# Keys and values of the memory attention, made within the input projection instead of among the scans

## The chip, the core and the metric

One core of one Trainium2 chip runs the whole kernel. The metric is the device time of one execution in microseconds; the time before is the median of three runs. TensorE multiplies matrices and has two levels of clock, 1.2 and 2.4 GHz; the profile gives what was granted as a share of the higher. VectorE (DVE in the rows), ScalarE (ACT) and GpSimd (POOL) do the elementwise work, SyncE (SP) issues most of the transfers. Each engine executes its instructions in an order that is fixed when the kernel is built, and waits by semaphores.

## The reference, cut to what matters

One layer of an encoder: 2048 tokens of width 1024. One input projection feeds a state space mixer (S5: per group of 16 channels a diagonal recurrence forwards and backwards over the sequence) and the queries of a cross-attention into 256 memory tokens. Both outputs go through one output projection and a layer norm, then through a mixture of 16 experts.

```python
def _memory_attention(q_mem, mem, w_kv):
    kv = (mem @ w_kv).reshape(bsz, mem.shape[1], 2, MEM_HEADS, MEM_HEAD_DIM)
    q = q_mem.reshape(bsz, L, MEM_HEADS, MEM_HEAD_DIM)
    s = jnp.einsum('blhd,bmhd->bhlm', q, kv[:, :, 0]) * (MEM_HEAD_DIM ** -0.5)
    p = jax.nn.softmax(s, axis=-1)
    out = jnp.einsum('bhlm,bmhd->blhd', p, kv[:, :, 1])
    return out.reshape(bsz, L, MEM_WIDTH)
...
proj = x @ s5_w_in[j]
mix = _s5_mixer(proj[..., :S5_WIDTH], ...)
mem_out = _memory_attention(proj[..., -MEM_WIDTH:], mem, mem_w_kv[i])
y = jnp.concatenate([mix, mem_out], axis=-1) @ w_out
```

The change concerns `mem @ w_kv`: 256 memory tokens by 1024, times 1024 by 512 (256 columns of keys, 256 of values). It depends on no token of the sequence.

## The kernel before, in words

Every float32 product is made of three f16 matmuls (`mm3`, L106 to L110): each operand is split into a high half (a cast, on ScalarE) and a low half (the difference to it). `split_w` (L90) makes the low half on VectorE, and scales a weight by 64 while it does so. `split_w_pool` (L95) does the same with ScalarE and GpSimd: a cast on ScalarE, a scaling in place on ScalarE, and a subtraction on GpSimd.

`front` runs these stages:

- **Input projection** (`inproj_u`): 16 tiles of 128 tokens. Per tile a load `xr` (SyncE), a cast `xh` (ScalarE), a difference `xl` (L262: GpSimd for tiles 1 to 5, VectorE otherwise), 24 matmuls into `pu` and 48 into `pq`, both with one PSUM buffer; `pu` is evicted by ScalarE (L281), `pq`, the queries, by ScalarE and VectorE (L294, L295, rows `OT<-pq`). The tables of the recurrence are made in between: `s5_base` behind tile 0, nearly all of it small VectorE instructions (names `b_...`, `pwa`, `turn`), `scan_base` behind tile 6 (names `E`), and `s5_block(b)` behind every second tile, on GpSimd (`wtmp`, L576) and VectorE (`wz` in PSUM, L580; `wi` and `wo`, L581). A block's kernel matrix goes through PSUM tag `pk`, which has one buffer, and ScalarE reads it out (L616, `ks<-pkk`). After tiles 7 and 15 the columns are transposed by TensorE into the chunk columns `U` (L301, evicted at L304 and L306). Before that, `U`'s memory takes the raw input weights. The `U` half of tiles 0 to 7 is written first, the other one after the last tile.
- **Scans**: eight blocks of four groups, in the order 6, 7, 0 to 5. `chunk_inputs(b)` multiplies `U` by stored matrices (L638, `pvv`) and ScalarE evicts them (L641, `S<-pvv`); `scan(b)` turns the states (`turn_states`: L690 on VectorE, L691 on GpSimd, L695 on either), scans them on VectorE (L715), turns them back, and ScalarE copies them out in eight instructions (L720, `SS<-S`). Behind the first two blocks stands `kv(att, t)`: it loads the memory (`mraw`, L347) and `w_kv` (`kraw`, L354) in pieces, splits them with ScalarE and VectorE (L348, L349, L91, L92), runs 96 matmuls, and writes keys and values as f16 halves `kh`, `kl`, `vh`, `vl` (L366 to L378).
- **Attention and S5 output**: the order on TensorE is written out by hand (`manual_schedule`, `STEPS`): the outputs of blocks 0 and 1, then attention steps (scores L734, exponentials L740 on ScalarE, probabilities, values) between the outputs of the other blocks.
- Then the gated unit, the output projection with norm and routing, and the experts.

Apart from TensorE's hand-written stage, the framework sets the order on each engine when the kernel is built: it walks through the program with a timeline of estimated durations and takes what is ready, the earlier in the program first. So an instruction can move past others on its engine, but on the chip that order doesn't change any more. Buffers of one PSUM tag are given out in program order. The lines ahead of the prediction's steps:

```python
for b in order[:KEEP]:
    self.scan(b)
self.kv(att, t)
...
for b in order[KEEP:]:
    self.chunk_inputs(b, [self.stored(b, q, wip) for q in range(GB // 2)], self.ps1, "s5")
    self.scan(b)
```

Of the kernel before, what the change touches and what calls it, by code (L numbers as in the profile page):

```python
# [18 lines left out]
P = 128  # L19
# [3 lines left out]
DC = 8  # L23
# [15 lines left out]
XG = 9  # L39
GTB = 1  # L40
GELU = 6

EARLY = 2
EARLY_T = 10
# [19 lines left out]
WS = 64.0  # L64
# [8 lines left out]
class Kern:  # L73
# [97 lines left out]
    def front(self, fr):  # L171
# [17 lines left out]
        with ExitStack() as s5:  # L189
            up = s5.enter_context(self.pool("up", side="left"))  # L190
            self.U = up.tile([P, 2, G, P], F32, name="U")
            att = s5.enter_context(self.pool("att", side="left"))
            with ExitStack() as t0:
                self.inproj_u(t0, scp)
            ssp = s5.enter_context(self.pool("ssp", side="left"))
            self.SS = ssp.tile([P, 2, G, P + 2], F32, name="SS")
            self.nc.gpsimd.memset(self.SS[:, 0, :, 0:1], 0.0)
            self.nc.gpsimd.memset(self.SS[:, 1, :, P + 1:P + 2], 0.0)
            with ExitStack() as t2:
                self.ps1 = t2.enter_context(self.pool("ps1", bufs=3, space=PSUM))  # L200
                self.ps2 = t2.enter_context(self.pool("ps2", bufs=1, space=PSUM))
                order = list(range(NB - KEEP, NB)) + list(range(NB - KEEP))
                gtp = t2.enter_context(self.pool("gtp", bufs=GTB, side="left"))
                wp = [t2.enter_context(self.pool("wopa", bufs=2, side="left"))]
                with ExitStack() as t:
                    self.scp = t.enter_context(self.pool("scm", bufs=2, side="right"))
                    for b in order[:KEEP]:
                        self.scan(b)
                    self.kv(att, t)
                    wip = t.enter_context(self.pool("wip", bufs=WIP, side="right"))  # L210
                    for b in order[KEEP:]:
                        self.chunk_inputs(b, [self.stored(b, q, wip) for q in range(GB // 2)], self.ps1, "s5")
                        self.scan(b)
                steps = self.attention(t2)
                gup = t2.enter_context(self.pool("gup", bufs=2, side="right"))
                wp.append(t2.enter_context(self.pool("wopb", bufs=2, side="right")))
                with self.tc.manual_schedule(engines={mybir.EngineType.PE}):
                    counts = iter(STEPS)
                    for b in range(NB):
                        if b == GELU:  # L220
                            self.glu_weights()
                        for _ in self.s5_out(b, gtp, wp, gup):
                            for _ in range(next(counts)):
                                next(steps, None)
                    for _ in steps:
                        pass
# [9 lines left out]
        self.xk = [keep.tile([P, D], F32, name=f"xk{e}") for e in range(EARLY)]  # L236
        self.outproj()

    def inproj_u(self, t0, scp):
# [15 lines left out]
        for t in range(NT):  # L255
# [52 lines left out]
            if t == 0:  # L308

                self.PRb = ps.tile([P, 16, 2, G], F32, tag="pw", bufs=1, name="PRb")  # L310
                self.s5_base(t0)
                nc.scalar.activation(self.PRb, self.PR[:, 1:17], AF.Copy)
                self.blkp = t0.enter_context(self.pool("s5blk", side="right"))
            if t == 6:
                self.scan_base(scp)
            if t % 2 == 1 and t < NT - 1:
# [15 lines left out]
                    f(n - k)  # L332
                yield

    def kv(self, att, t):
        nc, a = self.nc, self.a
        ps = self.ps2
        kp = t.enter_context(self.pool("kvp", bufs=2, side="right"))
        self.kh = att.tile([P, 4, 256], F16, name="kh")
        self.kl = att.tile([P, 4, 256], F16, name="kl")  # L340
        self.vh = att.tile([P, 2, 256], F16, name="vh")
        self.vl = att.tile([P, 2, 256], F16, name="vl")
        mh = kp.tile([P, DC, 256], F16, bufs=1, name="memh")
        ml = kp.tile([P, DC, 256], F16, bufs=1, name="meml")
        for c in range(0, DC, 4):
            m = kp.tile([P, 4, 256], F32, tag="raw", name=f"mraw{c}")
            nc.sync.dma_start(m, a["memT"][:, c:c + 4])  # L347
            nc.scalar.activation(mh[:, c:c + 4], m, AF.Copy)  # L348
            nc.vector.tensor_tensor(ml[:, c:c + 4], m, mh[:, c:c + 4], op=ALU.subtract)  # L349
        kacc = [ps.tile([P, 512], F32, tag="at", bufs=3, name=f"pk{k}") for k in range(2)]  # L350
        vacc = [ps.tile([P, 512], F32, tag="pS", bufs=2, name=f"pv{k}") for k in range(2)]
        for c2 in range(0, DC, 2):
            raw = kp.tile([P, 2, 512], F32, tag="raw", name=f"kraw{c2}")
            nc.sync.dma_start(raw, a["w_kv"][:, c2:c2 + 2])  # L354
            wh = kp.tile([P, 2, 512], F16, tag="kvh", bufs=1, name=f"kvh{c2}")
            wl = kp.tile([P, 2, 512], F16, tag="kvl", bufs=1, name=f"kvl{c2}")
            self.split_w(wh, wl, raw)
            for i in range(2):
                c = c2 + i
                ends = c == 0, c == DC - 1  # L360
                for k in range(2):
                    sl = slice(k * P, k * P + P)
                    self.mm3(kacc[k][:, :256], wh[:, i, sl], wl[:, i, sl], mh[:, c], ml[:, c], *ends)
                    self.mm3(vacc[k][:, :256], mh[:, c, sl], ml[:, c, sl], wh[:, i, 256:], wl[:, i, 256:], *ends)
        for k in range(2):
            nc.scalar.activation(self.vh[:, k], vacc[k][:, :256], AF.Copy, scale=1.0 / WS)  # L366
            nc.vector.scalar_tensor_tensor(self.vl[:, k], vacc[k][:, :256], 1.0 / WS, self.vh[:, k], op0=ALU.mult, op1=ALU.subtract)
            th = kp.tile([P, 2, 512], F16, tag="kvh", bufs=1, name=f"kth{k}")[:, 0, :256]
            tl = kp.tile([P, 2, 512], F16, tag="kvl", bufs=1, name=f"ktl{k}")[:, 0, :256]
            nc.scalar.activation(th, kacc[k][:, :256], AF.Copy, scale=1.0 / WS)  # L370
            nc.vector.scalar_tensor_tensor(tl, kacc[k][:, :256], 1.0 / WS, th, op0=ALU.mult, op1=ALU.subtract)

            for hh in range(2):
                r = slice(hh * 64, hh * 64 + 64)
                for half in range(2):
                    o = slice(half * 64, half * 64 + 64)
                    nc.scalar.activation(self.kh[o, k * 2 + hh], th[r], AF.Copy)
                    nc.scalar.activation(self.kl[o, k * 2 + hh], tl[r], AF.Copy)  # L378


    def s5_base(self, t0):
# [1210 lines left out]
```

## Time and profile before

| | |
|---|---|
| median of three runs (lowest, highest) | 1093.69 us (1084.93, 1095.92) |
| the profiled execution | 1091.53 us |
| its span in the profile | 1089.7 us |
| TensorE busy in the span | 899.5 us, 83% |
| VectorE | 828.3 us, 76% |
| ScalarE | 540.5 us, 50% |
| GpSimd | 535.3 us, 49% |

The shares are means over stages with different limits, so the rows below go by stage. The input projection runs from the start to about 226 us, the scans from there to 337 us, the attention to about 540 us. A row of the timeline has the start, the time that the instruction took, its engine, line, operation, what it writes from what, and in brackets how long its engine was idle before it and what ended that. A duration holds what the instruction was held up once it had begun, so the same shape can have two durations.

### The profile page before, as it was taken

How to read it: one execution, taken by the hardware profiler on the slowest of the kernel's cores; microseconds unless marked ns; L12 is line 12 of the kernel's file. 1: busy time of each engine (PE TensorE's matmuls, PEld its weight loads, DVE VectorE, ACT ScalarE, POOL GpSimd, SP SyncE). 2: the span in 40 equal slices, each digit the busy share in tenths (PEclk: the TensorE clock that was granted, in tenths of full speed). 3: DMA queues.
4: the chain of work that ended last, by engine and by line, in shares of the span. 5: the costliest groups of instructions: out<-in, count | busy, mean ns of one | idle time of the engine just before them, and what ended most of it. 6: DMA issues, size and time to landing. Idle time of an engine off the chain costs nothing. (4 is left out here: it accounts for less than half of the span.)

```text
span 1089.7 us, 18757 instructions
## 1 busy us (share of the span) xinstructions
PE 899.5 (83%) x7108; PEld 606.8 (56%) x7108; DVE 828.3 (76%) x1636; ACT 540.5 (50%) x1068; POOL 535.3 (49%) x379
## 2 busy tenths in 40 slices
PE   7777599985845999899999888698979987989880
PEld 4444465674734877444554447476657754755540
DVE  7999888969997666483585676467878787878774
ACT  5122243445748776477633312265656554746530
POOL 1475655426663331325945444525444566367454
PEclk9899799999887999999999987899999998999995
DMA  7113355275271422417736331476578669557531
GB/s 253 41 45 117 121 180 202 69 243 168 61 227 46 132 81 77 140 55 267 257 141 116 78 114 64 142 292 227 206 269 319 215 225 334 198 205 233 208 107 65
DMA packets 65199, 178.14 MB, mean 163 GB/s; under 512 B 15121, under 2 KB 33425, under 8 KB 57681
## 3 DMA queue, kind: packets, MB, share of 16 engines
q1 hardware_dynamic: 44800, 128.83, 36.2%
q0 software_dynamic: 20304, 48.07, 12.9%
q8 instruction: 57, 0.93, 0.3%
q14 instruction: 38, 0.30, 0.1%
HBM read 141.95 MB, written 58.49 MB: 184 GB/s over the span
## 5 line engine op out<-in xcount | busy, mean ns | idle before, releaser
L92 DVE SCALAR_TENSOR_TENSOR wl<-raw,wh 128x1024 f16<-128x1024 f32 x82 | 97.8, 1219 | 10.4 <-ACT wh L91 7.9
L91 ACT ACTIVATE wh<-raw 128x1024 f16<-128x1024 f32 x82 | 82.0, 1048 | 24.1 <-PE pg L109 13.8
L109 PE MATMUL pg<-xl,wh 128*128 128x288 f16 (+1 forms) x256 | 73.3, 288 | 3.0 <-DVE xl L1462 2.8
L110 PE MATMUL pg<-xh,wl 128*128 128x288 f16 (+1 forms) x256 | 73.3, 288 | 0.9 <-issue 0.9
L108 PE MATMUL pu<-xh,wh 128*128 128x288 f16 (+1 forms) x256 | 71.8, 283 | 2.4 <-DVE hl L1049 1.9
L108 PE MATMUL pg<-xh,wh 128*128 128x288 f16 (+1 forms) x256 | 73.5, 289 | 0.0
L1206 POOL DMA_INDIRECT xs<-xg,idxall x31 | 38.9, 1256 | 70.2 <-DVE xg L1499 40.9
L110 PE MATMUL pu<-xh,wl 128*128 128x288 f16 (+1 forms) x256 | 71.6, 282 | 1.5 <-issue 1.5
L109 PE MATMUL pu<-xl,wh 128*128 128x288 f16 (+1 forms) x256 | 71.6, 282 | 0.0
L109 PEld LDWEIGHTS <-wh 128*128 128x128 f16 x576 | 58.1, 101 | 19.0 <-issue 5.7
L108 PEld LDWEIGHTS <-wh 128*128 128x128 f16 x576 | 58.3, 101 | 18.5 <-issue 3.5
L110 PEld LDWEIGHTS <-wl 128*128 128x128 f16 x576 | 57.9, 101 | 17.5 <-issue 4.4
L108 PE MATMUL pq<-xh,S 128*128 128x128 f16 x256 | 51.0, 235 | 15.9 <-DVE OT L295 15.9
L743 POOL TENSOR_TENSOR pe<-pe,ri 128x1024 f32<-128x1024 f32 x16 | 30.3, 1895 | 55.5 <-DVE ri L742 38.8
L108 PE MATMUL pu<-winh,xh 128*128 128x512 f16 x128 | 49.7, 388 | 6.6 <-ACT winh L91 6.6
L1201 POOL DMA_INDIRECT xg<-x1d,idxall x31 | 37.9, 1222 | 32.9 <-DMA out_x<-xg,idxall 13.0
L108 PE MATMUL py<-wh,hh 128*128 128x512 f16 x120 | 45.9, 385 | 8.8 <-ACT hh L1048 4.6
L1462 DVE TENSOR_TENSOR xl<-pt,xh 128x512 f16<-128x512 f32 x60 | 39.5, 683 | 16.1 <-ACT xh L1461 10.1
L1461 ACT ACTIVATE xh<-pt 128x512 f16<-128x512 f32 x60 | 34.0, 592 | 35.8 <-PE pt L1458 29.5
L110 PE MATMUL pq<-xh,S 128*128 128x128 f16 x256 | 51.2, 235 | 0.4 <-DVE S L92 0.3
L1458 PE MATMUL pt<-ident,xg 128*128 128x128 f32 x240 | 37.8, 285 | 16.5 <-DVE xl L1462 7.6
L691 POOL TENSOR_TENSOR m<-S,R 128x1024 f32<-128x1024 f32 x10 | 30.4, 3045 | 42.0 <-DVE S L715 23.6
(471 smaller groups left out, 3163.6 us busy)
## 6 DMA issues: line engine op xcount, KB each, us to landing
raw<-in_w_gate SPq DMA_DIRECT2D x16, 1024.0 KB
raw<-in_w_up SPq DMA_DIRECT2D x16, 1024.0 KB
raw<-in_w_down SPq DMA_DIRECT2D x16, 1024.0 KB
xr<-in_xT SPq DMA_DIRECT2D x16, 512.0 KB
xs<-wo SPq DMA_DIRECT2D x16, 512.0 KB
wol<-xs SPq DMA_DIRECT2D x16, 512.0 KB
M<-kd SPq DMA_DIRECT2D x64, 128.0 KB
xres<-in_x SPq DMA_DIRECT2D x16, 512.0 KB
```

Of the source, the lines that this page charges most:

```text
L91: self.nc.scalar.activation(hi, raw, AF.Copy, scale=WS)
L92: self.nc.vector.scalar_tensor_tensor(lo, raw, WS, hi, op0=ALU.mult, op1=ALU.subtract)
L108: mm(ps, lh, rh, start=first, stop=False)
L109: mm(ps, lh, rl, start=False, stop=False)
L110: mm(ps, ll, rh, start=False, stop=last)
L691: Q.tensor_tensor(m[:, 1], S[:, :, 1::-1], tab(1), op=ALU.mult)
L743: nc.gpsimd.tensor_tensor(pe, pe, ri.unsqueeze(2).to_broadcast([P, 4, 256]), op=ALU.mult)
L1201: return self.nc.gpsimd.indirect_dma_start(out=out, out_offset=None, in_=src, in_offset=bass.IndirectOffsetOnAxis(ap=idx, axis=0))
L1206: st = self.nc.gpsimd.indirect_dma_start(out=self.xs, out_offset=bass.IndirectOffsetOnAxis(ap=si, axis=0), in_=z[:sz], in_offset=None, bou ...
L1458: nc.tensor.transpose(pt[:, i, off:off + sz], x[:sz, (d0 + i) * P:(d0 + i) * P + P], self.ident[:sz, :sz])
L1461: nc.scalar.activation(xh[:, ds_, :n], pt, AF.Copy)
L1462: nc.vector.tensor_tensor(xl[:, ds_, :n], pt, xh[:, ds_, :n], op=ALU.subtract)
```

## The change

`kv` becomes a generator of three steps and is called from `inproj_u`: a step at the end of tiles 2, 3 and 4. The first loads the whole memory and the weights of the values, splits the memory (cast on ScalarE, difference on GpSimd) and loads the weights of the keys over the raw memory. The second splits the weights of the values with `split_w_pool`, runs 48 matmuls into one buffer of tag `pk`, and makes `vh` and `vl` in one instruction each. The third does the same for the keys, and copies them to `kh` and `kl` in eight instructions instead of sixteen. All loads and halves lie in the memory of `U`, which has no pool of its own for them any more. Six differences of 128x1024 that were on VectorE are now on GpSimd; of the four instructions of VectorE that read a finished product out of PSUM, two of double width are left. The call among the scans goes.

```diff
+KV0 = 2
-                self.inproj_u(t0, scp)
+                self.inproj_u(t0, scp, att)
...
-                    self.kv(att, t)
...
+            if t == KV0:
+                keys = self.kv(att, ps)
+            if KV0 <= t < KV0 + 3:
+                next(keys)
             if t == 6:
                 self.scan_base(scp)
...
+    def kv(self, att, ps):
         nc, a = self.nc, self.a
-        ps = self.ps2
-        kp = t.enter_context(self.pool("kvp", bufs=2, side="right"))
+        flat = self.U.rearrange("p j g k -> p (j g k)")
+        half = lambda i: flat[:, 4096 + 1024 * i:5120 + 1024 * i].bitcast(F16).rearrange("p (c m) -> p c m", c=DC)
+        raws = [flat[:, o:o + 2048].rearrange("p (c m) -> p c m", c=DC) for o in (2048, 0)]
...
+        mh, ml, wh, wl = (half(i) for i in range(4))
+        nc.sync.dma_start(raws[0], a["memT"])
+        nc.sync.dma_start(raws[1], a["w_kv"][:, :, 256:512])
         for c in range(0, DC, 4):
-            m = kp.tile([P, 4, 256], F32, tag="raw", name=f"mraw{c}")
-            nc.sync.dma_start(m, a["memT"][:, c:c + 4])
-            nc.scalar.activation(mh[:, c:c + 4], m, AF.Copy)
-            nc.vector.tensor_tensor(ml[:, c:c + 4], m, mh[:, c:c + 4], op=ALU.subtract)
...
-            raw = kp.tile([P, 2, 512], F32, tag="raw", name=f"kraw{c2}")
-            nc.sync.dma_start(raw, a["w_kv"][:, c2:c2 + 2])
...
-            self.split_w(wh, wl, raw)
...
+            cs = slice(c, c + 4)
+            nc.scalar.activation(mh[:, cs], raws[0][:, cs], AF.Copy)
+            nc.gpsimd.tensor_tensor(ml[:, cs], raws[0][:, cs], mh[:, cs], op=ALU.subtract)
+        nc.sync.dma_start(raws[0], a["w_kv"][:, :, 0:256])
+        yield
+        for c in range(0, DC, 4):
+            cs = slice(c, c + 4)
+            self.split_w_pool(wh[:, cs], wl[:, cs], raws[1][:, cs])
+        pv = ps.tile([P, 2, 256], F32, tag="pk", bufs=1, name="pv")
         for k in range(2):
...
+            for c in range(DC):
+                self.mm3(pv[:, k], mh[:, c, sl], ml[:, c, sl], wh[:, c], wl[:, c], c == 0, c == DC - 1)
+        nc.scalar.activation(self.vh, pv, AF.Copy, scale=1.0 / WS)
+        nc.vector.scalar_tensor_tensor(self.vl, pv, 1.0 / WS, self.vh, op0=ALU.mult, op1=ALU.subtract)
+        yield
+        for c in range(0, DC, 4):
+            cs = slice(c, c + 4)
+            self.split_w_pool(wh[:, cs], wl[:, cs], raws[0][:, cs])
+        pk = ps.tile([P, 2, 256], F32, tag="pk", bufs=1, name="pkeys")
...
+                self.mm3(pk[:, k], wh[:, c, sl], wl[:, c, sl], mh[:, c], ml[:, c], c == 0, c == DC - 1)
+        th, tl = (x[:, 0:2] for x in (mh, ml))
+        nc.scalar.activation(th, pk, AF.Copy, scale=1.0 / WS)
+        nc.vector.scalar_tensor_tensor(tl, pk, 1.0 / WS, th, op0=ALU.mult, op1=ALU.subtract)
...
+                nc.scalar.activation(self.kh[o, hh::2], th[r], AF.Copy)
+                nc.scalar.activation(self.kl[o, hh::2], tl[r], AF.Copy)
+        yield
```

## Rows read from the trace of the kernel before

**Rows 1.** Stretches: busy PE, PEld, DVE, ACT, POOL (instructions), granted clock, DMA share, GB/s.

```profile
12.00:60.00 48.00, 37.76 (x299) 23.78 (x296) 46.55 (x162) 12.59 (x22) 21.00 (x19) 0.93 0.32 98
60.00:131.00 71.00, 51.29 (x453) 34.78 (x454) 66.49 (x97) 19.22 (x43) 49.79 (x38) 0.88 0.30 103
131.00:150.00 19.00, 17.21 (x155) 11.81 (x153) 16.50 (x28) 10.28 (x25) 9.92 (x6) 1.00 0.37 125
150.00:222.00 72.00, 70.96 (x597) 44.33 (x595) 60.80 (x91) 30.55 (x68) 32.37 (x17) 1.00 0.43 147
...
229.50:292.00 62.50, 42.91 (x550) 36.18 (x546) 58.81 (x64) 35.34 (x79) 39.19 (x16) 0.92 0.48 160
292.00:337.00 45.00, 20.11 (x84) 15.25 (x85) 39.56 (x56) 24.94 (x59) 25.37 (x10) 0.79 0.55 164
```

**Rows 2.** Waits of TensorE, 12 to 150 us: total, times, longest.

```profile
PE pq L108 <- DVE OT L295: 15.9, 7, 4.4
PE pkk L614 <- DVE wo L581: 7.0, 1, 7.0
```

**Rows 3.** Timeline where the scans end: ScalarE, then TensorE.

```profile
333.21 3.41 ACT L720 ACTIVATE SS<-S 64x256 f32<-64x256 f32 x8 [1.77 <-DVE S L695]
...
337.71 0.37 PE L734 MATMUL pS<-kh,OT 128*128 128x256 f16 x1 [16.10 <-ACT pe L740]
```

**Rows 4.** Groups by shape, 222 to 300 us: busy, mean ns, idle before.

```profile
L92 DVE SCALAR_TENSOR_TENSOR kvl<-kraw,kvh 128x1024 f16<-128x1024 f32 x4 | 9.1, 2283 | 0.0
...
L349 DVE TENSOR_TENSOR meml<-mraw,memh 128x1024 f16<-128x1024 f32 x2 | 2.4, 1226 | 2.6 <-ACT memh L348 2.6
...
L348 ACT ACTIVATE memh<-mraw 128x1024 f16<-128x1024 f32 x2 | 2.1, 1057 | 2.5 <-DMA mraw<-in_memT 2.4
...
L367 DVE SCALAR_TENSOR_TENSOR vl<-pv,vh 128x256 f16<-128x256 f32 x2 | 0.8, 408 | 0.0
```

**Rows 5.** Timeline: two of four `kvl` on VectorE, GpSimd beside the second.

```profile
237.77 1.20 DVE L92 SCALAR_TENSOR_TENSOR kvl<-kraw,kvh 128x1024 f16<-128x1024 f32 x1
...
246.76 3.37 DVE L92 SCALAR_TENSOR_TENSOR kvl<-kraw,kvh 128x1024 f16<-128x1024 f32 x1
...
245.66 3.39 POOL L691 TENSOR_TENSOR m<-S,R 128x1024 f32<-128x1024 f32 x1
```

**Rows 6.** Timeline of ScalarE: copies of states, first and fourth block (eighth: rows 3).

```profile
245.95 3.40 ACT L720 ACTIVATE SS<-S 64x256 f32<-64x256 f32 x8
...
288.39 3.42 ACT L720 ACTIVATE SS<-S 64x256 f32<-64x256 f32 x8
```

**Rows 7.** Timeline at the start of the scans: TensorE, ScalarE.

```profile
226.04 3.71 PE L638 MATMUL pvv<-U,wt 128*64 128x128 f32 x64
...
230.52 1.07 ACT L641 ACTIVATE S<-pvv 128x512 f32<-128x512 f32 x2
```

**Rows 8.** Timeline before 60 us: an `xl`, VectorE beside it, VectorE without.

```profile
43.33 2.16 POOL L262 TENSOR_TENSOR xl<-xr,xh 128x1024 f16<-128x1024 f32 x1
...
43.43 2.14 DVE L431 SCALAR_TENSOR_TENSOR b_poly<-b_poly,b_tt 128x64 f32<-128x64 f32 x1
...
33.62 0.23 DVE L431 SCALAR_TENSOR_TENSOR b_poly<-b_poly,b_st 128x64 f32<-128x64 f32 x1
```

**Rows 9.** Timeline of ScalarE: read-outs of `pk` for blocks 0, 1 and 2.

```profile
98.52 0.58 ACT L616 ACTIVATE ks<-pkk 128x496 f32<-128x496 f32 x1 [2.85 <-PE pkk L614]
...
131.54 0.58 ACT L616 ACTIVATE ks<-pkk 128x496 f32<-128x496 f32 x1 [6.38 <-issue]
...
143.01 0.59 ACT L616 ACTIVATE ks<-pkk 128x496 f32<-128x496 f32 x1 [0.42 <-PE pkk L614]
```

**Rows 10.** Groups by line, 150 to 222 us (columns of rows 4): `wz`.

```profile
L580 DVE TENSOR_TENSOR wzo<-XC,PRb 128x512 f32<-128x512 f32 x19 | 13.2, 694 | 0.6
```

**Rows 11.** Timeline of TensorE at full clock: matmuls of 256 columns.

```profile
342.40 0.27 PE L735 MATMUL pS<-kl,OT 128*128 128x256 f16 x1
342.51 0.27 PE L734 MATMUL pS<-kh,OT 128*128 128x256 f16 x1
```

More of the change, by code (lines that the diff above doesn't have):

```diff
@@ L237, in front, with inproj_u @@
         self.outproj()
-    def inproj_u(self, t0, scp):
+    def inproj_u(self, t0, scp, att):
         nc, a = self.nc, self.a
@@ L333, in attention_steps @@
                 yield
-    def kv(self, att, t):
+    def kv(self, att, ps):
         nc, a = self.nc, self.a
-        ps = self.ps2
-        kp = t.enter_context(self.pool("kvp", bufs=2, side="right"))
+        flat = self.U.rearrange("p j g k -> p (j g k)")
+        half = lambda i: flat[:, 4096 + 1024 * i:5120 + 1024 * i].bitcast(F16).rearrange("p (c m) -> p c m", c=DC)
+        raws = [flat[:, o:o + 2048].rearrange("p (c m) -> p c m", c=DC) for o in (2048, 0)]
         self.kh = att.tile([P, 4, 256], F16, name="kh")
@@ L342, in kv @@
         self.vl = att.tile([P, 2, 256], F16, name="vl")
-        mh = kp.tile([P, DC, 256], F16, bufs=1, name="memh")
-        ml = kp.tile([P, DC, 256], F16, bufs=1, name="meml")
+        mh, ml, wh, wl = (half(i) for i in range(4))
+        nc.sync.dma_start(raws[0], a["memT"])
+        nc.sync.dma_start(raws[1], a["w_kv"][:, :, 256:512])
         for c in range(0, DC, 4):
-            m = kp.tile([P, 4, 256], F32, tag="raw", name=f"mraw{c}")
-            nc.sync.dma_start(m, a["memT"][:, c:c + 4])
-            nc.scalar.activation(mh[:, c:c + 4], m, AF.Copy)
-            nc.vector.tensor_tensor(ml[:, c:c + 4], m, mh[:, c:c + 4], op=ALU.subtract)
@@ L350, in kv @@
-        kacc = [ps.tile([P, 512], F32, tag="at", bufs=3, name=f"pk{k}") for k in range(2)]
-        vacc = [ps.tile([P, 512], F32, tag="pS", bufs=2, name=f"pv{k}") for k in range(2)]
-        for c2 in range(0, DC, 2):
-            raw = kp.tile([P, 2, 512], F32, tag="raw", name=f"kraw{c2}")
-            nc.sync.dma_start(raw, a["w_kv"][:, c2:c2 + 2])
-            wh = kp.tile([P, 2, 512], F16, tag="kvh", bufs=1, name=f"kvh{c2}")
-            wl = kp.tile([P, 2, 512], F16, tag="kvl", bufs=1, name=f"kvl{c2}")
-            self.split_w(wh, wl, raw)
[L358 to L364, printed above, removed]
@@ L365, in kv @@
-        for k in range(2):
[L366 to L378, printed above, removed]
+            cs = slice(c, c + 4)
@@ new lines, in kv @@
+            nc.scalar.activation(mh[:, cs], raws[0][:, cs], AF.Copy)
[6 more added lines that the diff above has]
+        pv = ps.tile([P, 2, 256], F32, tag="pk", bufs=1, name="pv")
+        for k in range(2):
+            sl = slice(k * P, k * P + P)
+            for c in range(DC):
+                self.mm3(pv[:, k], mh[:, c, sl], ml[:, c, sl], wh[:, c], wl[:, c], c == 0, c == DC - 1)
@@ new lines, in kv @@
+        nc.scalar.activation(self.vh, pv, AF.Copy, scale=1.0 / WS)
[5 more added lines that the diff above has]
+        pk = ps.tile([P, 2, 256], F32, tag="pk", bufs=1, name="pkeys")
+        for k in range(2):
+            sl = slice(k * P, k * P + P)
+            for c in range(DC):
+                self.mm3(pk[:, k], wh[:, c, sl], wl[:, c, sl], mh[:, c], ml[:, c], c == 0, c == DC - 1)
@@ new lines, in kv @@
+        th, tl = (x[:, 0:2] for x in (mh, ml))
+        nc.scalar.activation(th, pk, AF.Copy, scale=1.0 / WS)
+        nc.vector.scalar_tensor_tensor(tl, pk, 1.0 / WS, th, op0=ALU.mult, op1=ALU.subtract)
+        for hh in range(2):
+            r = slice(hh * 64, hh * 64 + 64)
+            for half_ in range(2):
+                o = slice(half_ * 64, half_ * 64 + 64)
+                nc.scalar.activation(self.kh[o, hh::2], th[r], AF.Copy)
+                nc.scalar.activation(self.kl[o, hh::2], tl[r], AF.Copy)
```

## The prediction

> **What bounds the kernel now.** I read the table of stretches first [rows 1]. From 12 to 131 us VectorE is busy for 46.6 of 48 us and 66.5 of 71 us, while TensorE has about 30 us of idle time. From 150 to 222 us the two change places: TensorE 71.0 of 72 us, VectorE 60.8. These two stretches are the input projection. From 229.5 to 337 us come the scans, with the keys and values among them: VectorE 98.4 of 107.5 us, TensorE 63.0.
>
> Then the waits before 150 us [rows 2]: TensorE waits 15.9 us for VectorE to free the query accumulator, and 7.0 us at once for VectorE's `wo`. So until about 150 us a delay of VectorE delays everything, and TensorE, which executes in order, has nothing with which to catch up.
>
> Last, the hand-over to the attention [rows 3]: the last copies of states begin on ScalarE at 333.21 us and last 3.4, the first exponentials come behind them, and TensorE waits 16.1 us for these. What the scan stage saves therefore arrives in the attention in full, and behind it in a chain that is serial down to the experts.
>
> The profiled execution took 1091.5 us, 1.8 more than its span; the median of the three runs is 1093.7. The sum below goes against 1091.5.
>
> **What the scan stage gets back.** Removed there are four `kvl` on VectorE (9.1 us), two `meml` (2.4) and four subtractions from PSUM (two `vl`, 0.8, and two alike for the keys), 13.1 us in all [rows 4], beside matmuls, casts and DMAs on engines with idle time. A count of instructions misleads here, since `kvl` takes 1.20 us alone and 3.37 us beside a GpSimd instruction [rows 5]; in the second case the wait would hit the next VectorE instruction instead. So I take the rhythm of the blocks [rows 6]: ScalarE copies states out once for each of eight blocks. From the first block to the fourth, with the keys and values among them, 42.4 us pass, 14.15 a block; from the fourth to the eighth 44.8 us, 11.2 a block. Three blocks at 2.95 us less give 8.8. In the first block itself `kvl` at 237.77 us stands between the scans: 1.1. And ScalarE waited 2.4 us for `mraw` and cast it [rows 4] before it evicted the first chunk inputs, so that they were out at 231.6 us, though TensorE had done the second at 229.75 [rows 7]; with the usual 0.6 us for an eviction the first turn starts 1.3 us earlier. Together 11.2 us. Bounds: below, undisturbed durations alone, 4 x 1.2 + 4 x 0.4 + 1.3 = 7.7; above, all 13.1 and 1.3, 14.4.
>
> **What the projection pays on VectorE.** The new low halves are six GpSimd subtractions, 128x1024 to f16. The same shape stands there as `xl`, 2.16 us. Where it runs, VectorE's small instructions stop: a `b_poly` that takes 0.23 us took 2.14 beside one [rows 8]. So one costs VectorE about 1.9 us in this stretch. Memory columns and value weights have all they need as soon as their DMAs land, and GpSimd is busy for 21 of 48 us there [rows 1], so these four fall between some 20 and 60 us, where VectorE is full: 4 x 1.9 = 7.6. Bounds: 0, if they hit instructions that don't stop, and 8.6 (4 x 2.16).
>
> The two for the keys come later, since their f16 buffers are free only after the value matmuls, which wait for `pk`. That PSUM tag has one buffer, and the order written is block 0, values, block 1, keys, block 2; block 0 is read out at 98.52 us [rows 9]. After 100 us half of VectorE's work is `wz` and `wo` with an operand in PSUM. Later, where GpSimd is busy for 32.4 of 72 us [rows 1], 19 of them take 0.69 us in the mean [rows 10], so they hardly stop. Between 0 and 3.8 us I take 2.0. The two new VectorE subtractions read 128x512 from PSUM, the size of a `wz`: 1.4.
>
> The Trainium skill speaks against this part. Its page "Perfetto Trace Analysis", section "Optimizing Scalar/DVE Operations", says that an offload from VectorE to GpSimd may not help, since they share a port; "SBUF — State Buffer", section "Who interferes with whom", calls this an exclusive lock that a VectorE instruction with two SBUF inputs needs too. Taken as an account of that port alone, six instructions of 1.2 us are exchanged for six of 2.16: 5.8 us more, 1097.3, inside the forecast's own range. The trace agrees on the stopping (2.14 against 0.23 us, rows 8), but rhythm and start of the scan stage give more back than the port's share.
>
> **TensorE, ScalarE, SyncE.** 96 matmuls of 256 columns; at full clock they follow each other every 0.11 us [rows 11]: 5.3 us for values, 5.3 for keys. The values run after 98.5 us, where TensorE has idle time that VectorE makes (from 60 to 131 us 19.7 us, rows 1): nothing; without that cover 5.3. The keys follow block 1's read-out (131.54 us) and must be out before block 2's (143.01) [rows 9], where TensorE idles 1.8 us of 19 [rows 1]. VectorE's own delay opens more, so between 0 and 5.3 I take 2.0. ScalarE gets ten casts of about 1.05 us and ten evictions and copies of about 0.6 [rows 4, 9], 16.5 us, and is busy 32 of 119 us before 131 [rows 1]: nothing. SyncE gets three loads of 1 MB; the third waits for GpSimd, and behind it in SyncE's queue stand the loads of `xr`. The DMA share is 0.32 in that stretch [rows 1], and `xr` is loaded ahead: nothing; uncovered, one GpSimd wait, 2 us. `U` itself is written after tiles 7 and 15, the steps come at tiles 2 to 4: nothing.
>
> **The sum.** 1091.5 - 11.2 + 7.6 + 2.0 + 1.4 + 2.0 = 1093.3 us. All the gain goes again, as the projection is held by the very engine that was to be spared. With every bound on the good side 1077.1 (-14.4), on the bad side 1108.2 (-7.7 + 8.6 + 3.8 + 1.4 + 10.6).
>
> **Rivals.**
> *The projection takes it up (faster).* The GpSimd instructions hit VectorE instructions with an operand in PSUM, or wait themselves, and the matmuls fill TensorE's idle time; only 1.4 and 2.0 are left: 1083.7, and with the gain at its upper bound 1080.5. For it: 30 us of idle TensorE, and the 0.69 us of `wz`. Against it: the row on `b_poly`, and a VectorE with nothing else to run before 60 us than such small instructions.
> *The single `pk` buffer (slower).* Five users now follow each other where there were three, on four engines that execute in an order fixed beforehand. What this can do is seen at block 1: ScalarE stood 6.38 us for its matmuls [rows 9], which waited for `wo` [rows 2]. If values and keys each bring one more such stop, 12.8 us are added: 1106.1. It decides from 11 us of stops on. Against it: 33 us lie between the read-outs of blocks 0 and 1, and the values need 5.3 of them.
> *The gain was not there.* If VectorE and GpSimd hand turns to each other and `kvl` only filled the gaps, a half of it, 5.6 us, comes back: 1098.9. Against it: VectorE idles only 3.7 us of 62.5 in that stretch [rows 1].
>
> **How the numbers follow.** Forecast 0.47 (its own range 1086 to 1100), taken up 0.26, the `pk` buffer 0.17, no gain 0.10. From 1079 to 1107 lie all but the ends of the first two rivals. A measurement of this kernel can tell about 1%, 1082.8 and 1104.6 around the median. Of the taken-up case some six tenths lie below, of the forecast a tenth: 0.21. Of the `pk` case seven tenths lie above, of the last a fifth, of the forecast a tenth: 0.19. The rest, 0.60, is no change that can be told.
>
> **What the profile would show.** Right: first copies of states of the eighth block some 91 to 96 us after the first chunk inputs are evicted (now 102.7), 11.2 us a block throughout; the last transposes into `U` 10 to 16 us later than 226 us; `b_` instructions of 2 us beside `ml` and `wl` on GpSimd; value matmuls right behind block 0's read-out, with no longer wait behind them. Wrong: the projection ends by 232 us (taken up), or later than 245 with ScalarE or TensorE standing at `pk` (the single buffer), or the blocks don't come faster.

## The result: slower by 1.3%

The changed kernel takes 1106.26 us (median of four runs, 1102.61 to 1107.82), the kernel before, measured beside it, 1093.06 us: 1.0127 times, with a 95% interval of 1.0081 to 1.0172, or 13.2 us more. The prediction said 1093.3 us and no change that can be told. The profiled execution took 1106.92 us, its span is 1105.1 (before 1091.53 and 1089.7).

The stretches of the changed kernel, columns as in [rows 1]:

```profile
12.00:60.00 48.00, 34.96 (x292) 22.49 (x290) 44.95 (x158) 17.57 (x26) 23.61 (x20) 0.86 0.46 157
60.00:131.00 71.00, 55.44 (x474) 36.85 (x472) 68.57 (x95) 22.59 (x47) 57.09 (x41) 0.95 0.24 79
131.00:150.00 19.00, 15.16 (x144) 11.99 (x144) 15.49 (x24) 11.01 (x25) 11.40 (x7) 0.91 0.54 185
150.00:222.00 72.00, 68.89 (x551) 44.24 (x552) 57.05 (x84) 29.29 (x61) 33.14 (x17) 0.95 0.42 141
222.00:245.00 23.00, 21.68 (x225) 15.78 (x224) 13.85 (x22) 10.06 (x23) 3.11 (x2) 1.00 0.39 127
```

TensorE stands 3.8 us of 19 and 3.1 us of 72 idle in the third and fourth stretch, where it had 1.8 and 1.0 before [rows 1]. The projection isn't over at 222 us. ScalarE's timeline shows its end, the start of the scans and the hand-over to the attention:

```profile
240.86 0.60 ACT L306 ACTIVATE U<-ptu 128x512 f32<-128x512 f32 x1 [0.81 <-PE ptu L301]
...
243.77 0.60 ACT L650 ACTIVATE S<-pvv 128x512 f32<-128x512 f32 x1 [2.31 <-PE pvv L647]
...
258.20 1.69 ACT L729 ACTIVATE SS<-S 64x256 f32<-64x256 f32 x4
...
348.36 3.41 ACT L729 ACTIVATE SS<-S 64x256 f32<-64x256 f32 x8 [6.41 <-POOL S L704]
351.78 0.47 ACT L749 ACTIVATE pe<-pS,nm 128x256 f32<-128x256 f32 x1
```

The first and the last of these lines in the kernel before:

```profile
225.39 0.60 ACT L306 ACTIVATE U<-ptu 128x512 f32<-128x512 f32 x1 [0.75 <-PE ptu L301]
...
336.64 0.47 ACT L740 ACTIVATE pe<-pS,nm 128x256 f32<-128x256 f32 x1
```

ScalarE's last eviction into `U` began at 225.39 us before and begins at 240.86 now: 15.5 us later. From there to the first exponential 110.9 us pass; before it was 111.2 (336.64 - 225.39). The scan stage, rid of 13.1 us of VectorE instructions [rows 4], has not become shorter. From the first eviction of chunk inputs to the eighth block's copies there are 104.6 us, before 102.7 [rows 3, 7].

In three stages the span's 15.4 us are +15.5 for the projection, -3.9 from its end to ScalarE's last f16 half of the gated unit, `mh` (264.8 us after it now, 268.6 before), and +3.8 for what follows (599.5 now, 595.7 before). That last part lay between 589 and 603 us in the profiled executions of the eight kernels below that compute the same, so no cause is looked for there.

### The profile page after: what moved, and what is told of

Read it like the earlier page. It is cut to its first block, busy times and chain, and to the rows that moved or that the text cites. A ratio compares the mean times of both kernels' runs of the same rounds, so it can differ in the third digit from the quotient of the medians.

```text
span 1105.1 us, 18780 instructions
## 1 busy us (share of the span) xinstructions
PE 898.8 (81%) x7108; PEld 608.9 (55%) x7108; DVE 825.4 (75%) x1628; ACT 541.2 (49%) x1062; POOL 554.4 (50%) x385
## 5 line engine op out<-in xcount | busy, mean ns | idle before, releaser
L109 PE MATMUL pq<-xh,S 128*128 128x128 f16 x256 | 49.9, 233 | 22.4 <-DVE OT L295 22.4
L109 PE MATMUL py<-wh,hh 128*128 128x512 f16 x120 | 47.2, 393 | 15.9 <-DVE xg L1508 9.5
L1508 DVE SCALAR_TENSOR_TENSOR xg<-py,idxall,xg 128x512 f32<-128x512 f32 x60 | 43.2, 744 | 19.3 <-DMA xg<-xs,idxall 14.6
L585 POOL TENSOR_TENSOR wtmpo<-YC,PI 128x1024 f32<-128x1024 f32 x16 | 32.8, 2049 | 39.8 <-DVE wi L590 35.5
L111 PE MATMUL pq<-xh,S 128*128 128x128 f16 x256 | 49.8, 232 | 0.0
L110 PE MATMUL pq<-xl,S 128*128 128x128 f16 x256 | 49.7, 232 | 0.0
L110 PE MATMUL pu<-winl,xh 128*128 128x512 f16 x128 | 49.3, 386 | 0.3 <-DVE winl L93 0.3
```

What stands on the lines that cost most here:

```text
L109: mm(ps, lh, rh, start=first, stop=False)
L110: mm(ps, lh, rl, start=False, stop=False)
L111: mm(ps, ll, rh, start=False, stop=last)
L585: Q.tensor_tensor(t[:, :, 0:n], ch(y, all_, n), pw(self.PI, lo, d, all_, n), op=ALU.mult)
L1508: nc.vector.scalar_tensor_tensor(xg[:sz, hs], py[:sz], gate, xg[:sz, hs], op0=ALU.mult, op1=ALU.add, **acc)
```

## The experiments

Two questions: what makes the projection late, and where the scan stage's gain is. The first column of numbers is the begin of ScalarE's last eviction into `U`; the second what that is above the kernel without the keys' and values' work; the third the time from there to the attention's first exponential; the last the time against the kernel before, with its interval.

| kernel | end of projection | above no work | to first exponential | times before |
|---|---|---|---|---|
| before | 225.4 | 1.0 | 111.2 | 1 |
| changed | 240.9 | 16.4 | 110.9 | 1.0127 (1.0081 to 1.0172) |
| e1 without the work | 224.4 | 0 | 110.7 | 0.9981 (0.9954 to 1.0007) |
| e2 low halves on VectorE | 239.9 | 15.4 | 111.0 | 1.0153 (1.0103 to 1.0203) |
| e3 the transposes' ring | 233.8 | 9.3 | 110.2 | 1.0080 (1.0054 to 1.0107) |
| e4 at tiles 4 to 6 | 240.0 | 15.5 | 110.9 | 1.0111 (1.0072 to 1.0150) |
| e5 12 of 96 products | 235.2 | 10.7 | 111.1 | 1.0116 (1.0070 to 1.0162) |
| e6 products alone | 239.1 | 14.6 | 109.8 | 1.0156 (1.0119 to 1.0192) |
| e7 no work, GELU late | 224.8 | 0.3 | 104.9 | 1.0038 (0.9991 to 1.0085) |
| e8 before, `kvl` four times | 224.1 | -0.3 | 130.4 | 1.0209 (1.0155 to 1.0262) |
| e9 all at tile 1 | 241.4 | 17.0 | 111.1 | 1.0168 (1.0124 to 1.0212) |
| e10 the same, on VectorE | 233.2 | 8.7 | 111.1 | 1.0052 (1.0022 to 1.0082) |
| e11 no subtractions | 231.2 | 6.8 | 110.9 | not comparable |
| e12 at tile 1, no subtractions | 226.2 | 1.8 | not used | not comparable |

The last two change what the experts are given, which makes that part some 70 to 90 us longer; of them only the projection counts. The kernel before was measured anew beside each set of runs, and its median lay between 1084.5 and 1093.1 us, so the ratios compare and the times don't. The columns in us come from one profiled execution each. The kernel before and e8 have the same projection, and their ends lie 1.3 us apart, so a difference of that size tells nothing. Most expectations count to the end of VectorE's last copy into `U`, 1.4 to 1.7 us later (242.6 us in the changed kernel).

### Without the work at all (e1)

```python
for n, shape in (("kh", [P, 4, 256]), ("kl", [P, 4, 256]), ("vh", [P, 2, 256]), ("vl", [P, 2, 256])):
    setattr(self, n, att.tile(shape, F16, name=n))
    self.nc.gpsimd.memset(getattr(self, n), 0.0)
```

> The changed kernel without the keys and values at all: their loads, casts, subtractions, products and copies are left out, and the four tiles kh, kl, vh, vl are filled with zeros at the start, so the memory attention works on nothing. What it tells: the price of the work in either place. Projection: if the work itself makes the projection late, the last eviction of the chunk columns is back at 226 us (242.6 with the work); if something else in the new build did, it stays above 235. Scan stage, from the first copy of states to the last block's first copy to the state array (102.7 us before, 104.6 after): theory 'no gain to have' (the work ran in gaps that VectorE and GpSimd leave each other when they take turns) expects 100 to 105 us and a kernel of about 1087 to 1091 us, hardly under the kernel before; theory 'gain eaten' (the gain of about 11 us was there, but the late projection and the order of the queues ate it) expects 91 to 96 us and about 1078 to 1082 us.

The projection is back at 224.4 us: the work itself makes it late. The kernel takes 1091.71 us beside 1092.82 for the one before. In the place where they stood before, keys and values cost at most half a per cent. The scan stage of this kernel is that of the changed one: counted from the first eviction of chunk inputs, each block's copies begin at the same time within 0.05 us:

```profile
227.09 0.60 ACT L603 ACTIVATE S<-pvv 128x512 f32<-128x512 f32 x1 [2.07 <-PE pvv L600]
...
331.72 3.41 ACT L682 ACTIVATE SS<-S 64x256 f32<-64x256 f32 x8 [6.41 <-POOL S L657]
335.15 0.47 ACT L702 ACTIVATE pe<-pS,nm 128x256 f32<-128x256 f32 x1
```

104.6 us again. So the late projection did not eat a gain; there was none to see at the hand-over. Its first scans show how VectorE and GpSimd share the time (VectorE's timeline, then GpSimd's):

```profile
229.47 1.22 DVE L652 TENSOR_TENSOR m<-S,R 128x1024 f32<-128x1024 f32 x1 [3.62 <-ACT S L603]
232.96 1.29 DVE L657 TENSOR_TENSOR S<-m 128x512 f32<-128x512 f32 x2 [2.26 <-POOL m L653]
234.17 2.63 DVE L677 TENSOR_TENSOR_SCAN S<-decay,S 128x128 f32<-128x128 f32 x8
...
229.52 3.41 POOL L653 TENSOR_TENSOR m<-S,R 128x1024 f32<-128x1024 f32 x1 [16.43 <-ACT S L603]
```

The two products of a turn start together, and GpSimd's ends 3.46 us later, about the sum of VectorE's 1.2 and of the 2.35 that this instruction takes where nothing holds it (at 272.79 us in the same kernel, where it was four scans of VectorE beside it that were held, 3.51 us in place of 1.36). They take turns, and VectorE waits 2.26 us for the other's end. In the kernel before a `kvl` stood in such a wait with 3.37 us, GpSimd beside it [rows 5].

### Where the scan stage's gain went (e7, e8)

In the changed kernel as in e1, VectorE's order has the first GELU instructions and the splitting of the gated unit's weights ahead of the last block's turning. From the changed kernel's VectorE:

```profile
338.80 0.67 DVE L834 SCALAR_TENSOR_TENSOR gu<-gu,trg 128x512 f32<-128x512 f32 x1
339.40 1.35 DVE L724 TENSOR_TENSOR_SCAN S<-decay,S 128x128 f32<-128x128 f32 x4
340.68 1.86 DVE L93 SCALAR_TENSOR_TENSOR E<-E 128x512 f16<-128x512 f32 x3
342.46 1.21 DVE L699 TENSOR_TENSOR S<-S,R 128x1024 f32<-128x1024 f32 x1
343.60 0.68 DVE L93 SCALAR_TENSOR_TENSOR E<-E 128x512 f16<-128x512 f32 x1
```

In the kernel before those four `E<-E` ran at 341.16 us, eight microseconds behind the start of the last copies of states. In e7 (the work left out as in e1) a copy of a few numbers of the last states stands ahead of them, and of the first GELU:

```python
nc.scalar.activation(raw[:, 0, 0:4], self.SS[:, 1, b * GB:b * GB + GB, 1], AF.Copy)
...
nc.scalar.activation(u[:, 0:4], self.SS[:, 1, b * GB:b * GB + GB, 1], AF.Copy)
```

> The kernel without the keys' and values' work, with six GELU instructions of 0.6 us and four subtractions for the GLU weights (2.5 us) kept behind the last block's turning, by a copy of a few numbers of the last states ahead of them; without that, VectorE has them ahead of it (312.95 to 328.2 us). Theory 'taking turns, and the gain eaten': in the scan stage VectorE's and GpSimd's instructions exclude one another, so that it lasts as long as the sum of both alone; then the 6 us that the missing work leaves were filled by these ten instructions, and with them out of the way the time from the last eviction of the chunk columns to the first exponential of the attention falls from 110 to 104 us, and the kernel takes about 1086 us. Theory 'no gain to have': the stage is bound by a chain that neither piece of work lengthens, 109 to 110 us and 1091 to 1092 us.

The last block's end on VectorE, and on ScalarE the first, fourth and eighth block's copies:

```profile
319.39 2.62 DVE L677 TENSOR_TENSOR_SCAN S<-decay,S 128x128 f32<-128x128 f32 x8
322.04 1.22 DVE L652 TENSOR_TENSOR S<-S,R 128x1024 f32<-128x1024 f32 x1
325.49 0.69 DVE L657 TENSOR_TENSOR S<-S 128x512 f32<-128x512 f32 x1 [2.23 <-POOL S L653]
...
241.84 1.69 ACT L682 ACTIVATE SS<-S 64x256 f32<-64x256 f32 x4
...
282.52 1.70 ACT L682 ACTIVATE SS<-S 64x256 f32<-64x256 f32 x4 [0.30 <-POOL S L657]
...
326.22 3.41 ACT L682 ACTIVATE SS<-S 64x256 f32<-64x256 f32 x8 [4.52 <-DVE S L657]
329.66 0.47 ACT L702 ACTIVATE pe<-pS,nm 128x256 f32<-128x256 f32 x1
```

To the first exponential 104.9 us pass, 5.8 fewer than in e1 and 6.3 fewer than before. So the work was worth 6.3 us in the scan stage, and the order built without it spends that on ten instructions of later stages. But the kernel gained nothing by it: 1087.69 us beside 1084.50 for the one before (the 1086 us expected were thought of beside some 1092), 1.0038 times, no better than e1. The lead is gone a few tiles on: of the 5.8 us against e1, 1.0 are left at the first exponential of tile 3. The ten instructions run behind the hand-over instead, which would account for it. From the projection's end to the first exponential of tile 14 there are 181.2 us in e7, 180.9 in e1, 180.9 in the changed kernel, and 184.7 before. So 3.5 to 3.9 us are what comes out of the attention, whichever of these orders is taken.

> The kernel before with each of the four low-half subtractions of the keys' and values' weights (128x1024) made four times over, twelve more in all. Theory 'taking turns': each costs the 1.1 us that it takes alone, so the scan stage grows by 12 to 14 us and the kernel takes about 1106 us. Theory 'gaps': they run while VectorE would wait for GpSimd, and the kernel stays under 1098 us. The profiled mean of 2.28 us for each, taken as their price, would give 27 us and 1120 us.

```python
self.split_w(wh, wl, raw)
for _ in range(3):
    nc.vector.scalar_tensor_tensor(wl, raw, WS, wh, op0=ALU.mult, op1=ALU.subtract)
```

All three numbers missed. The stretch grew by 19.1 us (130.4, before 111.2). Of these 2.5 are the four `E<-E`, which the order of this kernel has ahead of the hand-over (at 332.51 us); the rest is 1.4 us for each of the twelve. Groups by shape, 225 to 355 us:

```profile
L359 DVE SCALAR_TENSOR_TENSOR kvl<-kraw,kvh 128x1024 f16<-128x1024 f32 x12 | 19.9, 1658 | 0.0
L92 DVE SCALAR_TENSOR_TENSOR kvl<-kraw,kvh 128x1024 f16<-128x1024 f32 x4 | 9.2, 2288 | 0.0
```

"Gaps" falls: they are paid for, each with its 1.2 us alone and a little more. That the first four had used up the gaps would fit, but isn't shown: what they cost can't be read from the price of the next twelve.

### What makes the projection late (e5, e6, e11)

> The changed kernel with 12 of the 96 matrix products of the keys and values: only the first of the eight chunks is multiplied, so keys and values are wrong sums; loads, casts, all six subtractions, evictions and copies stay. Theory 'TensorE is the projection's bound': 84 products of 256 columns at 0.11 us are 9.2 us, and the waits for the one read-out buffer get shorter too; the last eviction of the chunk columns comes at 228 to 233 us (242.6 with all, 225.1 without any of the work), the kernel at 1092 to 1098 us. Theory 'held VectorE': the six subtractions are still there, so the end stays at 240 to 243 us and the kernel at 1104 to 1107 us.

```python
for c in (0,):
    self.mm3(pv[:, k], mh[:, c, sl], ml[:, c, sl], wh[:, c], wl[:, c], True, True)
```

> The changed kernel without the six subtractions on GpSimd: the low halves are left out, and the products take the high halves in their place, as many products as before; loads, casts, evictions and copies stay. Theory 'held VectorE': the six holds (8 us early, 4 us for the keys) are the larger part, and the last eviction of the chunk columns comes at 230 to 235 us instead of 242.6, the kernel at 1.002 to 1.006 times the one before. Theory 'TensorE's backlog': 96 products alone, in this place, give 239.8 us, so the end is at 238 to 242 us, and the kernel at 1.010 to 1.015 times.

```python
nc.scalar.activation(wh[:, cs], raws[1][:, cs], AF.Copy, scale=WS)
nc.scalar.activation(raws[1][:, cs], raws[1][:, cs], AF.Copy, scale=WS)
```

Without 84 products the end comes 5.7 us earlier, without the six subtractions 9.7, without anything 16.4. Both theories are in it, and the six subtractions have the larger part. How they hold VectorE stands in the trace of the changed kernel (VectorE, then GpSimd, then ScalarE):

```profile
21.13 6.74 DVE L440 SCALAR_TENSOR_TENSOR b_poly<-b_poly,b_st 128x64 f32<-128x64 f32 x5
...
28.92 2.43 DVE L416 TENSOR_SCALAR b_ts<-b_tt 128x64 f32<-128x64 f32 x4
...
39.48 2.15 DVE L440 SCALAR_TENSOR_TENSOR b_poly<-b_poly,b_tt 128x64 f32<-128x64 f32 x1
...
23.56 4.21 POOL L355 TENSOR_TENSOR U<-U 128x1024 f16<-128x1024 f32 x2
...
29.03 2.17 POOL L99 TENSOR_TENSOR U<-U 128x1024 f16<-128x1024 f32 x1 [1.25 <-DVE b_tt L421]
...
39.43 2.12 POOL L99 TENSOR_TENSOR U<-U 128x1024 f16<-128x1024 f32 x1 [6.10 <-ACT U L98]
...
69.00 1.03 ACT L312 ACTIVATE PRb<-PR 128x1024 f32<-128x1024 f32 x1 [6.27 <-DVE PR L498]
```

And in e11, where GpSimd's subtractions are missing:

```profile
21.52 3.08 DVE L441 SCALAR_TENSOR_TENSOR b_poly<-b_poly,b_st 128x64 f32<-128x64 f32 x5
...
25.65 0.49 DVE L417 TENSOR_SCALAR b_ts<-b_tt 128x64 f32<-128x64 f32 x4
...
59.97 1.03 ACT L312 ACTIVATE PRb<-PR 128x1024 f32<-128x1024 f32 x1 [0.45 <-DVE PR L499]
```

3.66 us for the first two, 1.83 each, 1.94 for the third, and 1.9 for the fourth (2.15 us for an instruction of 0.23 [rows 8]): 7.5 us for the four that run before 60 us. The table that VectorE makes there, `PRb`, is ready at 69.0 us, against 59.8 to 60.3 in the kernel before, in e1 and in e11. What e11 doesn't separate is the hold of VectorE from GpSimd's own time and from products that wait for their low halves.

A lower granted clock is not the cause. The changed kernel had 0.91 and 0.95 from 131 to 222 us, behind the idle times of TensorE shown above, where the kernel before had 1.00 [rows 1]; so for part of that time it had the lower of the two levels, 1.2 GHz. But e4 had 1.00 in both stretches, and 0.86 and 0.93 in the two ahead of them (before: 0.93 and 0.88), and its projection ends at 240.0 us all the same.

> The kernel without the keys' and values' work, to which only 96 products of the same shape are given back in the projection, at tiles 6 and 7, made of tiles that are there anyway (the inputs' and the query weights' halves), with the one-buffer read-out tile and one eviction for each 48; no load, no cast, no subtraction; the memory attention works on what they leave. Theory 'TensorE is the projection's bound': the last eviction of the chunk columns moves from 225.1 to 234 to 237 us, the kernel from 1091.7 to 1101 to 1104 us. Theory 'held VectorE': it stays at 225 to 228 us, 1092 to 1095 us.

```python
if t in (6, 7):
    pv = ps.tile([P, 2, 256], F32, tag="pk", bufs=1, name=f"pv{t}")
    for k in range(2):
        for c in range(DC):
            self.mm3(pv[:, k], xh[:, c], xl[:, c], wqh[:, c], wql[:, c], c == 0, c == DC - 1)
    nc.scalar.activation(self.vh if t == 6 else self.vl, pv, AF.Copy, scale=1.0 / WS)
```

The same number of products cost 14.6 us here, more than their 10.5 at full clock. The order put them at 138 to 150 us, and from 131 to 222 us TensorE is then busy for 90.8 of 91 us: nothing is left to absorb them. Where the other 4.1 come from is open. The order ahead of them is another one too: from 60 to 131 us TensorE made 362 matmuls at a granted clock of 0.80, in e1 465 at 0.88. So the price of a product hangs on where it runs, and this run doesn't give it for the places of the changed kernel.

### Where the products run (e3, e4, e9, e10, e12)

The product groups of the changed kernel (count; shortest, median, longest in ns; begin of the first and of the last), values and keys, and ScalarE around them:

```profile
L109 PE MATMUL pv<-U x16: 272/273/421, 118.1 to 124.1; 128*128 128x256 f16 x16
...
L109 PE MATMUL pkeys<-U x16: 272/272/273, 133.1 to 138.0; 128*128 128x256 f16 x16
```

```profile
111.88 0.58 ACT L625 ACTIVATE ks<-pkk 128x496 f32<-128x496 f32 x1 [0.79 <-PE pkk L623]
...
123.33 1.06 ACT L97 ACTIVATE U<-U 128x1024 f16<-128x1024 f32 x1 [5.55 <-PE pv L111]
...
138.52 0.60 ACT L378 ACTIVATE U<-pkeys 128x512 f16<-128x512 f32 x1 [5.28 <-PE pkeys L111]
```

The values' operands are ready at 42 us, when GpSimd ends their last subtraction. Their products wait until ScalarE has read block 0 out of the one `pk` buffer, which stands first in the program. The keys' come when the third block's kernel rows and the first transposes are due.

> The changed kernel with the two product tiles (pv and pkeys) in the two-buffer ring of the transposes instead of the one buffer of the read-outs. Theory 'TensorE's stops': the stops for the one buffer go, the read-outs of the kernels' rows no longer wait for the values' and keys' evictions, and the last eviction of the chunk columns comes 3 us or more earlier (239 or less); time about 1102. Theory 'held VectorE': no change, 242 to 243, 1105 to 1107 us.

```python
pv = ps.tile([P, 2, 256], F32, tag="tr", bufs=2, name="pv")
```

The end comes 7.1 us earlier than in the changed kernel, more than twice what was expected at least. The values now run at 101 to 110 us, the keys at 129 to 137. Whether the earlier place or the freed buffer does more, this run alone does not tell.

> The changed kernel with the three parts of the work at tiles 4, 5 and 6 instead of 2, 3 and 4, so that the first subtractions no longer fall on the polynomials of the state-space base (21 to 43 us). Theory 'held VectorE, early': the read-out PRb is back from 69.0 to about 60 to 62 us, and the 8 us of the first holds go through to the end: last eviction at about 235 us, time about 1098. Theory 'TensorE's stops': the early 8 us are made up by the third read-out anyway (it came only 3.6 us later), and the key products now stand nearer to the first transposes: last eviction at 242 to 248 us, time 1106 to 1112.

```python
KV0 = 4
```

Nothing was moved where it mattered: GpSimd's two `ml` ran at 24.04 us (23.56 before the edit), `PRb` was read out at 69.6 us as in the changed kernel (69.0), and the end is within 0.9 us. The loads land early, and the order takes what is ready. A later place in the program is no later place on the engine, and the theories were not told apart.

> The changed kernel with the six low-half subtractions on VectorE instead of GpSimd (and without the three-step form: ScalarE then casts once and VectorE multiplies and subtracts in one instruction). Theory 'held VectorE' (a GpSimd subtraction of 2.15 us holds VectorE for about 1.9 us): the same halves cost VectorE 1.2 us each, and ScalarE four casts less, so the last eviction of the chunk columns comes 4 to 6 us earlier, 237 to 239 us, and the kernel takes about 1101 us. Theory 'TensorE's stops' (the one buffer of the read-outs, and the key products in front of the first transposes): VectorE has slack where it matters, and the end stays within 1 us of 242.6, the time at 1105 to 1107 us.

```python
nc.vector.tensor_tensor(ml[:, cs], raws[0][:, cs], mh[:, cs], op=ALU.subtract)
...
self.split_w(wh[:, cs], wl[:, cs], raws[1][:, cs])
```

Only 1.0 us earlier, which is no difference between two traces. The keys' products came 8 us later than in the changed kernel (141.4 us), where TensorE has nothing to spare; so the run mixes two things. The next two keep the products out of the way, with all three parts at tile 1, ahead of block 0 in the program:

```python
KV0 = 1
...
if t == KV0:
    for _ in self.kv(att, ps):
        pass
```

> The changed kernel with all three parts of the work at tile 1, that is, ahead of the first block's kernel rows in the program. In the changed kernel the values' product tile takes the one buffer of the kernel rows' read-outs after the first of these, so its 48 products, whose operands are ready at about 42 us, run at 118 to 124 us, and the keys' 48 at 133 to 138 us; here they have the buffer first. Theory 'place of the products': TensorE has over 20 us of idle time between 12 and 131 us and none to spare after it, so products at 45 to 80 us cost nothing, and what is left is the share of the casts and subtractions, at most the 10.7 us that the run with few products showed: last eviction of the chunk columns at 230 to 236 us, kernel 1.003 to 1.009 times the one before. Theory 'held VectorE': now all six subtractions fall where VectorE sets the pace, and the end comes no earlier than 240 us, 1.011 times or more.

> The same with the six low-half subtractions on VectorE (1.2 us each) instead of GpSimd (2.15 us each, in which VectorE is held). Theory 'place of the products': 0 to 5 us earlier than with GpSimd, since where TensorE does not set the pace VectorE does, last eviction at 229 to 234 us, kernel 1.000 to 1.007 times the one before. Theory 'held VectorE': 240 us becomes 235 us, 1.006 to 1.009 times.

With GpSimd, "place of the products" fails by 5.4 us: 241.4, as "held VectorE" had it. With VectorE it holds: 233.2, and 1.0052 times the time before; but the exchange of the engines brought 8.2 us, where 0 to 5 were expected. TensorE's waits of e9, 20 to 131 us, say why place alone is not enough (total, times, longest):

```profile
PE pq L109 <- DVE OT L295: 14.3, 2, 12.4
PE pu L111 <- DVE xl L262: 7.6, 1, 7.6
PE pkeys L109 <- DVE vl L366: 6.3, 1, 6.3
```

The first of these stands in e10 too (18.1 us, longest 14.3), the other two don't: the products, moved ahead, wait for VectorE in TensorE's queue, and the tiles wait behind them. The keys run at 66 to 81 us; in e10 at 47 to 52.

> All three parts of the work at tile 1, without the six low-half subtractions (the products take the high halves in their place, 96 as before, so keys and values are less exact and the expert part behind runs with other loads); loads, casts, products, two subtractions from PSUM, evictions and copies stay. With the subtractions on VectorE in this place the last eviction of the chunk columns by ScalarE began at 233.2 us, without any of the work at 224.4. Theory 'VectorE's instructions alone': of these 8.7 us the six subtractions (1.2 us each) are 7.2 and the two from PSUM 1.4, and 96 products at 30 to 52 us cost nothing; the eviction begins at 224.5 to 227 us. Theory 'products cost even here': 229 us or later. The time of the whole kernel says nothing here.

226.2 us, 1.8 above no work. So casts, 96 products, copies and the two VectorE subtractions from PSUM cost 1.8 us in this place, and 6.8 in the changed kernel's (e11). The six subtractions cost 9.7 us at the changed kernel's place (240.9 - 231.2), 15.2 at tile 1 on GpSimd (241.4 - 226.2, 2.5 each), and 7.0 there on VectorE (233.2 - 226.2, 1.2 each, the undisturbed duration in [rows 5]).

## Why the prediction was wrong

**Scan stage, 11.2 us back: the step that failed.** It read the blocks' rhythm in [rows 6] as two rates, 14.15 us a block with the work and 11.2 without, and took three times the difference, 8.8. The slower rate was not the work's. Without any of the work, and with the order kept (e7), the first three intervals take 40.7 us, 13.6 a block, and the last four 43.7, 10.9 a block; with it they took 42.4 and 44.8. The early blocks are slow and the later ones fast in either kernel, for a reason that no run here looks into, and the work makes up 1.7 us of the difference where 8.8 were counted. The rest of what it cost there is 1.1 us in the last four blocks, 1.0 in the first block (1.1 predicted) and 2.5 between the last eviction into `U` and the first chunk inputs (1.3 predicted). That is 6.3 us together, below the prediction's lower bound of 7.7 from undisturbed durations, which it stated and set aside. With the order that was built, 0.3 us of it show at the hand-over, and 3.9 at tile 14 of the attention.

**"What the scan stage saves arrives in the attention in full"** [rows 3]: a delay does (the 15.5 us of the projection stand at the first exponential as 15.1), a saving did not. e7's 5.8 us against e1 were gone at tile 14, and 2.8 of the 3.9 us that the changed kernel does win stand at tile 3, where the kernel before has most of the ten instructions still to do; that it is these is likely, but not shown. The prediction did not ask what VectorE would be given to do in the time set free.

**Holds, 7.6 and 2.0 us: right.** The six cost 9.7 us at the projection's end, and the trace shows 7.5 us of holds for the four early ones. Of the keys' two, the one at 125.55 us stopped nothing (VectorE's instructions beside it took their usual 0.7 us), and the one at 132.37 held a `ks` of 0.17 us for 1.56. The Trainium skill's "Perfetto Trace Analysis", section "Optimizing Scalar/DVE Operations", says that such an offload might not help. The trace agrees: at tile 1 GpSimd's six cost 8.2 us more than VectorE's own, and at the changed kernel's place, where the products moved too (e2), 1.0. The account made from the page alone was 5.8 us; it counted the port, and not what stands behind it in TensorE's queue.

**Products and subtractions from PSUM, 2.0 and 1.4 us: too small.** All that isn't the six subtractions costs 6.8 us in the changed kernel and 1.8 at tile 1. The prediction had seen that the values would run behind block 0's read-out, and priced this at nothing because of idle time up to 131 us. There TensorE waits for VectorE in order [rows 2], and the products did not fill those waits: from 12 to 150 us those for the query accumulator came to 21.0 us (15.9 before, 18.0 in e1). That loads and casts cost nothing holds to within the 1.8 us.

**The rivals.** "The gain was not there" carried a chance of 0.10 and is the one that the runs bear out, with 6.3 us in e7 and 3.9 in the kernel as it was built, where it named 5.6; its time of 1098.9 was too low all the same. The argument against it, that VectorE idles only 3.7 us of 62.5, used a busy time that contains waiting for GpSimd. "The single `pk` buffer" named the time almost to the microsecond (1106.1), but that is luck: its sum kept the scan stage's 11.2 us. Its stops are only a part: the ring of e3 gives 7.1 us back, the subtractions 9.7. Both stops stand in the trace, 5.55 and 5.28 us on ScalarE, while TensorE itself waited at the buffer only 1.9 us. "Taken up" is out: the projection ended at 241 us, not by 232. Of the prediction's signs, the end of the projection (15.5 us later, 10 to 16 named) and the `b_` instructions of 2 us came; of the signs of being wrong, "the blocks don't come faster" did: 104.6 us to the eighth block's copies, where 91 to 96 were named.

**The sum with the measured terms:** projection +9.7 and +6.8, less 1.0 by which the kernel before already ended later than the one without the work, makes 15.5; less 3.8 to 3.9 from the scans to the gated unit, 11.6. The median rose by 13.2; the 1.6 between lie within the interval. The forecast was 1.8 more than before. Of the 9.8 us between that and 11.6 the scan stage makes up 7.3 (11.2 - 3.9), products and subtractions from PSUM 3.4 (6.8 - 3.4), the holds 0.1, and the 1.0 goes off. With 3.9 us to win and 7.8 to pay against the kernel before in the best form found (e10, 233.2 - 225.4), no place in the projection that was tried beats it.

## What to carry to other kernels

Where two engines take turns, the busy time of each contains waiting; before a stage is promised to shrink, price the work at its undisturbed duration, and run the kernel once with the work left out, for that is all that moving it can bring. Then ask what the freed engine will be given next: here ten instructions of later stages took the place. In the stage that receives the work, an instruction costs what it costs on the engine that sets the pace there, and a matmul is free only if the buffer order in the program lets it run where TensorE idles.

## What was not expected of the hardware

- The hold goes both ways. GpSimd's 128x1024 product takes 2.35 us where nothing holds it, 3.4 beside one VectorE instruction, and 5.58 where VectorE has several in a row ready (the changed kernel at 340.90 us, beside the VectorE rows shown above).
- The same GpSimd subtraction cost 1.6 us of the projection on average at tiles 2 to 4 and 2.5 at tile 1, more than its own 2.15; on VectorE it cost 1.2.
- In the no-work kernel VectorE reads as busy for 90.2 of 107 us of the scan stage and in the kernel before for 97.9 of 106; that difference of 7.7 us made 0.5 us at the hand-over.
